# The second feed-forward block's opening tile, half of it in three passes of rounded parts

## The chip, the cores and the metric

The kernel runs on one core of a Trainium2 chip. The metric is the device time of one execution in microseconds (us), taken as the median of several runs. The engines named below are TensorE (PE; its weight loads are listed apart as PEld), VectorE (DVE), ScalarE (ACT), GpSimd (POOL), and SyncE (SP), which here only issues DMA transfers.

## The reference

One inference step of a decoder trunk with one layer: a half-step SwiGLU feed-forward block, a mixer, a second half-step feed-forward block, and a final RMS norm. The width is 1024 features, the hidden width 2816, and 520 tokens go through it (512 of a prompt and 8 single new tokens). Cut to what matters here:

```python
h = h + 0.5 * swiglu(rms_norm(h, ffn1_norm), w1_gate, w1_up, w1_down)
m, states = hybrid_mixer(rms_norm(h, mix_norm), ...)      # ends in  cat @ w_out
h = h + m
h = h + 0.5 * swiglu(rms_norm(h, ffn2_norm), w2_gate, w2_up, w2_down)
y = rms_norm(h, final_norm)
# swiglu(x, wg, wu, wd) = (silu(x @ wg) * (x @ wu)) @ wd
```

All of it is float32.

## The kernel before

**Layout.** Activations lie with features on the 128 partitions: the residual `h` is eight blocks of 128 features by 520 tokens, and the tokens are cut into two halves of 260. So a matmul has a 128x128 weight and moves 260 columns.

**Two kinds of matmul.** Most products are made of rounded parts. A float32 value is split into a rounded part in the type float32r and the rest, also in float32r: ACT makes the first by a copy with a cast, DVE the second by a subtraction (`part`, L250, for activations; `split`, L134, for weights). A product is then three matmuls that add up in PSUM: high weight by high activation, high by low, low by high (`mm3`, L150). A plain product (`plain`, L299) is one float32 matmul of the program on the unsplit values; the trace shows it as two instructions on PE.

**The feed-forward blocks** (`class Ffn`, L271). A hidden tile f is 128 columns of the gate weight and 128 of the up weight. Most tiles are computed by `product` (L470), seven products of sums of quarters instead of eight. They need the activations as seven combinations per pair of feature blocks (j, j+4), j from 0 to 3, each in two parts. For a pair, `scaled` (L229) writes `xg`, four slots of 260 tokens: slots 0 and 3 are the two token halves of block j, slots 1 and 2 those of block j+4. `prep_pair` (L255) makes three DVE instructions of sums (`sums4`, L237: L238, L240, L242), then the parts of slots 0 to 2 in one ACT and one DVE instruction over 780 columns, and the parts of the four sums `xd` over 1040 columns. All go to `xth` and `xtl`; slot 3 itself is not split.

**The opening tile.** The second block's tile 0 (`direct` is 1) is computed by `plain` instead, straight from `xg`, while the mixer's last output projection still runs. Per pair that is eight float32 products: gate and up, block j and block j+4, two token halves. Its gate and up banks are PSUM tiles of the tag BE. Its two weights lie unsplit in one of two 1 MB places `raw`, loaded by `plain_load` (L287). When all four pairs are done, `keep` (L317) copies the banks out.

**The order.** The end of the mixer is written as `LAST_PLAN`, "h0 h2 h1 n0 h3 n1 n2 n3". An `h` step (`wout`, L1292) adds the output projection to two feature blocks of `h`: twelve matmuls to a PSUM bank (eight L160, four L165), one bank per block and token half, two banks in rotation, each added to `h` by one DVE instruction (L1310). As each feature block is complete, `fin` (L782) squares it, and once block j+4 is there it calls `scaled` for pair j. An `n` step (`fill`, L791) emits the eight plain products of pair j and `prep_pair` for that pair. Beyond that, the build works out a fixed order for each engine: it plays the program through on a timeline of its own and lets an instruction that is ready go ahead of an earlier one that is not, unless a line pins it (`keep_in_program_order`, `issue_after`, `high_priority`). So the matmuls of the `n` steps stand between those of the `h` steps on PE.

**After it.** `scales` (L558) makes the token norms, `plain_out` (L365) closes tile 0, and `stream` (L561) runs tiles 1 to 21 and the down projections; for each of them ACT casts and DVE subtracts the weight parts (L139, L141, L396, L400).

Of the kernel before, what the change touches and what calls it, by code (L numbers as in the profile page):

```python
# [10 lines left out]
F32 = mybir.dt.float32  # L11
F32R = mybir.dt.float32r
AF = mybir.ActivationFunctionType
ALU = mybir.AluOpType
# [3 lines left out]
P = 128  # L18
# [4 lines left out]
HB = NT // 2  # L23
HALVES = (slice(0, HB), slice(HB, NT))
KD = D // P
# [43 lines left out]
def tile_trunk_step(ctx: ExitStack, tc: tile.TileContext, ins: dict, outs: dict):  # L69
    nc = tc.nc  # L70
# [7 lines left out]
    tmp = ctx.enter_context(tc.tile_pool(name="tmp", bufs=2, side="right"))  # L78
# [32 lines left out]
    half, ends, added = [], [], []  # L111
# [38 lines left out]
    def mm3(ps, whi, wlo, xhi, xlo, start, stop, pin=False, **kw):  # L150
        first = nc.tensor.matmul(ps, whi, xhi, start=start, stop=False, **kw)  # L151
        if pin:
            tc.keep_in_program_order(first)
        nc.tensor.matmul(ps, whi, xlo, start=False, stop=False, **kw)  # L154
        nc.tensor.matmul(ps, wlo, xhi, start=False, stop=stop, **kw)  # L155
# [11 lines left out]
    def ws(w, k, m=P):  # L167
        return w[:, k * m : (k + 1) * m]
# [60 lines left out]
    def scaled(cell, norm, j, name, halves=False):  # L229
        xg = cell(f"xg_{name}{j}")  # L230
        for d, out in ((j, xg[:, 0::3]), (j + KD // 2, xg[:, 1:3])):
            hd = h[:, d].rearrange("p (b t) -> p b t", b=2)
            for s in (slice(0, 1), slice(1, 2)) if halves else (slice(0, 2),):
                nc.scalar.activation(out=out[:, s], in_=hd[:, s], func=AF.Copy, scale=v(norm, d))
        return xg

    def sums4(xg, xd):  # L237
        nc.vector.tensor_tensor(out=xd[:, 0:2], in0=xg[:, 0::2], in1=xg[:, 3:4].to_broadcast([P, 2, HB]),  # L238
                                op=ALU.subtract)
        nc.vector.scalar_tensor_tensor(out=xd[:, 2], in0=xd[:, 1], scalar=-1.0, in1=xg[:, 0], op0=ALU.mult,  # L240
                                       op1=ALU.subtract)
        return nc.vector.scalar_tensor_tensor(out=xd[:, 3], in0=xd[:, 2], scalar=-1.0, in1=xg[:, 1], op0=ALU.mult,  # L242
                                              op1=ALU.subtract)
# [6 lines left out]
    def part(hi, lo, s):  # L250
        cast = nc.scalar.copy(hi, s)
        low = nc.vector.tensor_tensor(out=lo, in0=s, in1=hi.bitcast(F32), op=ALU.subtract)  # L252
        return cast.ins, low.ins

    def prep_pair(nx, cell, xg, j, name, late=None):  # L255
        xth, xtl, _, _ = nx
        xd = cell(f"xd_{name}{j}")
        last = sums4(xg, xd)

        def parts(s, t):  # L260
            return part(xth[:, j, t], xtl[:, j, t], s)

        parts(xg[:, 0:3], slice(0, 3))
        if late is not None:
            late.append(lambda: parts(xd, slice(3, 7)))
            return None
        return last.ins, *parts(xd, slice(3, 7))
# [3 lines left out]
    class Ffn:  # L271
# [15 lines left out]
        def plain_load(self, f, j=None, us=(0, 1), queue=nc.sync):  # L287
# [3 lines left out]
            for u in us:  # L291
# [4 lines left out]
                     for t in (self.raw[f][:, u], src[2 * f + u]))  # L296
                queue.dma_start(out=next(q), in_=next(q))

        def plain(self, f, xg, j, us=(0, 1), pin=False):  # L299
            for u in us:  # L300
                if (f, u) not in self.banks:
                    n = f"P{self.i}_{f}{u}"
                    if f == 1 and u == 0:
                        bs = [ps[0].tile([P, 512], F32, tag="A", bufs=2, name=f"{n}{b}") for b in range(2)]
                    else:
                        t = ps[0].tile([P, 2, 512], F32, tag="BE", bufs=2, name=n)
                        bs = [t[:, 0], t[:, 1], t]
                    self.banks[f, u] = bs
                for q in range(2):
                    for b, slot in enumerate(((0, 1), (3, 2))):  # L310
                        mm = nc.tensor.matmul(self.banks[f, u][b][:, :HB], ws(self.raw[f][:, u], j + 4 * q),  # L311
                                              xg[:, slot[q]], start=j == q == 0, stop=j == 3 and q == 1,
                                              skip_group_check=True)
                        if pin and q == b == 0:
                            tc.keep_in_program_order(mm)

        def keep(self, f, us):  # L317

# [395 lines left out]
    for j in range(KD // 2):  # L714
# [10 lines left out]
        last = j == KD // 2 - 1  # L725
# [44 lines left out]
    f2 = {}  # L770
# [11 lines left out]
    def fin(d, b, hs):  # L782
# [5 lines left out]
        if j >= 0 and b:  # L788
            f2[j] = scaled(cell2, "ffn2_norm", j, "f2")

    def fill(j):  # L791
        if not j:
            f2["ffn"].plain_load(0)
        f2["ffn"].plain(0, f2[j], j)
        last = j == KD // 2 - 1
        if last:
            with tc.high_priority():
                f2["ffn"].keep(0, (0,))
        f2["ends"] = prep_pair(f2["ffn"].nx, cell2, f2[j], j, "f2")
        if last:  # L800
            with tc.high_priority(), tc.issue_after(f2["ends"][1]):
                f2["copied"] = f2["ffn"].keep(0, (1,))
# [14 lines left out]
    last = act.tile([P, NT], F32, tag="acc", name="acc_last")  # L817
# [674 lines left out]
```

## Time and profile before

| | |
|---|---|
| median of three runs | 953.77 us (952.30 to 954.88) |
| the profiled execution, its own time | 953.41 us |
| its span, first to last instruction | 951.6 us |
| mean granted TensorE clock | 0.997 |
| PE busy | 941.0 us, 7674 matmuls |
| DVE busy | 850.9 us |
| ACT busy | 635.8 us |
| POOL busy | 152.5 us |

The span is read in stages: the first block, the mixer, and the second block from about 613 us on. The stage of the change is the stretch from 575 to 615 us, in which the mixer's last output projection and tile 0 share PE. A line number in a row of the profile is a line of the kernel. In a row of the timeline the columns are the start, the duration, the engine, the line, the operation and what it writes from what it reads; a bracket gives the idle time of the engine before it and what ended that. In the chain of waits the second column is the time that a piece adds to the chain.

### The profile page before, as it was taken

The numbers are of one execution on the slowest core, as the hardware profiler recorded it, in microseconds if no ns is written. First come the engines' busy times: TensorE is split into PE (matmuls) and PEld (weight loads), VectorE is DVE, ScalarE is ACT, GpSimd is POOL, SyncE is SP. The second block draws the span as 40 slices with busy tenths as digits, with TensorE's granted clock in tenths as the row PEclk, the third lists the DMA queues.
The fourth block names the chain that finished last, engine by engine and source line by source line (L and its number), as shares of the span: only waits on it lengthen the run. The fifth ranks groups of instructions, "written<-read, shape, count | busy, mean of one in ns | idle before, by whom it ended". The sixth has DMA issues, their size and how long they took to land.

```text
span 951.6 us, 19687 instructions
## 1 busy us (share of the span) xinstructions
PE 941.0 (99%) x7674; PEld 923.0 (97%) x7674; DVE 850.9 (89%) x1462; ACT 635.8 (67%) x1178; POOL 152.5 (16%) x230
## 2 busy tenths in 40 slices
PE   9999999999999999999999999999999999999996
PEld 8999999999999999999999999999999999999996
DVE  6899899998988698779989998999999999999986
ACT  7787757677566466474768745677776676776764
POOL 0011100100000002146252000112112101122120
PEclk9999999999999999999999999999999999999998
DMA  7676554455553334264365443447766655766652
GB/s 213 179 164 151 145 148 137 117 140 155 136 154 95 86 98 160 91 185 134 97 179 160 122 124 111 124 122 172 174 154 179 167 135 147 175 189 176 158 174 91
DMA packets 54123, 138.36 MB, mean 145 GB/s; under 512 B 7878, under 2 KB 16006, under 8 KB 54030
## 3 DMA queue, kind: packets, MB, share of 16 engines
q1 hardware_dynamic: 40046, 104.20, 34.3%
q0 software_dynamic: 13712, 32.78, 18.5%
q8 instruction: 60, 0.98, 0.4%
q14 instruction: 33, 0.27, 0.1%
q10 hardware_dynamic: 272, 0.13, 0.0%
HBM read 129.74 MB, written 7.34 MB: 144 GB/s over the span
## 4 chain that ended last, share of the span: by engine, by line
PE 79%; DVE 8%; DMA 5%; issue 4%; ACT 2%; POOL 1%; SPq 0%; DVEq 0%; POOLq 0%; ACTq 0%
PE A L160 7%; PE BE L160 6%; PE P L311 4%; PE wo L160 4%; PE A L151 4%; PE A L155 4%; PE A L154 4%; PE A L165 4%; PE BE L165 3%; PE BE L151 3%; PE BE L154 3%; PE BE L155 3%; PE wo L165 2%; PE inz L151 1%; DMA raw<-in_w2gu 1%
## 5 line engine op out<-in xcount | busy, mean ns | idle before, releaser
L504 ACT COPY ac<-A 128x260 f32<-128x260 f32 x85 | 31.7, 373 | 35.8 <-PE A L165 18.1
L433 DVE TENSOR_TENSOR s<-raw 128x1024 f32<-128x1024 f32 x39 | 47.5, 1219 | 5.5 <-DMA raw<-in_w2gu 3.3
L504 ACT COPY ac<-BE 128x260 f32<-128x260 f32 x41 | 15.4, 377 | 33.6 <-PE BE L165 17.9
L151 PE MATMUL inx<-xh_mx,whi_inx 128*128 128x260 f32 x112 | 31.8, 284 | 0.0
L154 PE MATMUL inx<-xl_mx,whi_inx 128*128 128x260 f32 x112 | 31.6, 282 | 0.0
L155 PE MATMUL inx<-xh_mx,wlo_inx 128*128 128x260 f32 x112 | 31.6, 282 | 0.0
L1033 DVE SCALAR_TENSOR_TENSOR A<-U,h,A 128x544 f32<-128x544 f32 x36 | 28.7, 797 | 1.5 <-ACT A L1031 1.1
L311 PE MATMUL P<-x,raw 128*128 128x260 f32 x128 | 28.8, 384 | 0.2 <-DMA raw<-in_w1gu 0.2
L311 PEld LDWEIGHTS P<-x,raw 128*128 128x128 f32 x128 | 24.2, 190 | 4.3 <-DMA raw<-in_w1gu 0.6
L160 PE MATMUL wo<-catg,whi_wo 128*128 128x260 f32 x192 | 27.5, 286 | 0.4 <-DVE h L1310 0.4
L1199 ACT ACTIVATE so<-br,sxdt 128x128 f32<-128x128 f32 x64 | 22.7, 376 | 4.5 <-DVE room L1201 3.2
L160 PEld LDWEIGHTS wo<-catg,whi_wo 128*128 128x128 f32 x192 | 24.8, 188 | 0.8 <-DVE h L1310 0.6
L139 ACT CAST thi<-raw 128x1024 fp32r<-128x1024 f32 (+1 forms) x14 | 14.2, 1013 | 15.6 <-PE wo L160 4.8
L1310 DVE TENSOR_TENSOR h<-wo,h 128x260 f32<-128x260 f32 x48 | 19.2, 420 | 5.5 <-PE wo L165 5.3
L252 DVE TENSOR_TENSOR gs<-gq,gs 128x780 fp32r<-128x780 f32 (+1 forms) x28 | 23.1, 826 | 0.0
L151 PE MATMUL inz<-xh_mx,whi_inz 128*128 128x260 f32 x80 | 22.9, 286 | 0.0
L154 PE MATMUL inz<-xl_mx,whi_inz 128*128 128x260 f32 x80 | 22.7, 283 | 0.0
L155 PE MATMUL inz<-xh_mx,wlo_inz 128*128 128x260 f32 x80 | 22.6, 283 | 0.0
L151 PEld LDWEIGHTS inx<-xh_mx,whi_inx 128*128 128x128 f32 x112 | 21.1, 188 | 0.2 <-issue 0.2
L160 PE MATMUL A<-xth_f,qs 128*128 128x260 f32 x84 | 21.2, 283 | 0.0
L160 PE MATMUL A<-xtl_f,qs 128*128 128x260 f32 x84 | 21.2, 284 | 0.0
L155 PEld LDWEIGHTS inx<-xh_mx,wlo_inx 128*128 128x128 f32 x112 | 21.1, 188 | 0.0
(3135 smaller groups left out, 4373.4 us busy)
## 6 DMA issues: line engine op xcount, KB each, us to landing
raw<-in_w2gu SPq DMA_DIRECT2D x44, 512.0 KB, 4.4
raw<-in_w1gu SPq DMA_DIRECT2D x41, 512.0 KB, 4.3
raw<-in_w_in SPq DMA_DIRECT2D x24, 512.0 KB, 3.5
raw<-in_w1d SPq DMA_DIRECT2D x16, 512.0 KB, 5.0
raw<-in_w2d SPq DMA_DIRECT2D x16, 512.0 KB, 4.6
raw<-in_w_out SPq DMA_DIRECT2D x12, 512.0 KB, 3.6
ab<-scr_acs SPq DMA_DIRECT2D x8, 512.0 KB, 5.9
h<-in_state_ssm SPq DMA_DIRECT2D x16, 256.0 KB, 3.9
```

Of the source, the lines that this page charges most:

```text
L151: first = nc.tensor.matmul(ps, whi, xhi, start=start, stop=False, **kw)
L154: nc.tensor.matmul(ps, whi, xlo, start=False, stop=False, **kw)
L155: nc.tensor.matmul(ps, wlo, xhi, start=False, stop=stop, **kw)
L160: mm = nc.tensor.matmul(ps, w, x, start=start, stop=False, **kw)
L165: nc.tensor.matmul(ps, w, xhi[k], start=False, stop=k == len(wlo) - 1, **kw)
L252: low = nc.vector.tensor_tensor(out=lo, in0=s, in1=hi.bitcast(F32), op=ALU.subtract)
L311: mm = nc.tensor.matmul(self.banks[f, u][b][:, :HB], ws(self.raw[f][:, u], j + 4 * q), xg[:, slot[q]], start=j == q == 0, stop=j == 3 and ...
L433: nc.vector.tensor_tensor(out=s1, in0=diag, in1=up0, op=ALU.add)
L504: self.copied = nc.scalar.copy(keep, out[:, :HB]).ins
L1033: nc.vector.scalar_tensor_tensor(out=A[:, :n], in0=U[:, j : j + n], scalar=w(j), in1=A[:, :n], op0=ALU.mult, op1=ALU.add)
L1199: nc.scalar.activation(out=o[:, q], in_=br, func=AF.Copy, scale=sxdt[:, j, b : b + 1]))
L1310: nc.vector.tensor_tensor(out=h[:, d, hs], in0=ps[:, :HB], in1=h[:, d, hs], op=ALU.add)
```

## The change

For pairs 0 and 1 the eight products of tile 0 become products of rounded parts; pairs 2 and 3 stay plain. Five things change in the program:

- `weight_parts` splits the first two 128-blocks of each weight quarter (a tile of 128x4x256) into `w0h` and `w0l`: one ACT cast and one DVE subtraction over 1024 columns, right behind the load.
- For pairs 0 and 1 `prep_pair` stands ahead of the products instead of behind them, since the products now read `xth` and `xtl` for slots 0 to 2.
- Slot 3 gets parts of its own, `x3h` and `x3l` (260 columns each, tag `ta`, of which there are two buffers in all).
- `parts_plain` makes the eight products with `mm3`: 24 float32r matmuls for the pair, into the same banks.
- `plain_banks` is the allocation of the banks, taken out of `plain`.

```diff
+        def parts_plain(self, f, w, x3, j):
+            self.plain_banks(f, (0, 1))
+            for u in range(2):
+                for q in range(2):
+                    wh, wl = (t[:, 2 * u + q, j * P : j * P + P] for t in w)
+                    for b, slot in enumerate(((0, 1), (3, 2))):
+                        xh, xl = x3 if slot[q] == 3 else (t[:, j, slot[q]] for t in self.nx[:2])
+                        mm3(self.banks[f, u][b][:, :HB], wh, wl, xh, xl, j == q == 0, False, skip_group_check=True)
+
         def plain(self, f, xg, j, us=(0, 1), pin=False):
+            self.plain_banks(f, us)
+            for u in us:
+                for q in range(2):
+                    for b, slot in enumerate(((0, 1), (3, 2))):
+                        mm = nc.tensor.matmul(self.banks[f, u][b][:, :HB], ws(self.raw[f][:, u], j + 4 * q),
+                                              xg[:, slot[q]], start=j == q == 0, stop=j == 3 and q == 1,
+                                              skip_group_check=True)
+                        if pin and q == b == 0:
+                            tc.keep_in_program_order(mm)
+
+        def plain_banks(self, f, us):
             for u in us:
                 if (f, u) not in self.banks:
...
                     self.banks[f, u] = bs
-                for q in range(2):
-                    for b, slot in enumerate(((0, 1), (3, 2))):
-                        mm = nc.tensor.matmul(self.banks[f, u][b][:, :HB], ws(self.raw[f][:, u], j + 4 * q),
-                                              xg[:, slot[q]], start=j == q == 0, stop=j == 3 and q == 1,
-                                              skip_group_check=True)
-                        if pin and q == b == 0:
-                            tc.keep_in_program_order(mm)
...
+    def weight_parts():
+        src = f2["ffn"].raw[0].rearrange("p u (q c) -> p (u q) c", q=2)[:, :, : 2 * P]
+        hi, lo = (f2["xg"].tile([P, 4, 2 * P], F32R, tag=t, name=t) for t in ("w0h", "w0l"))
+        nc.scalar.copy(hi, src)
+        nc.vector.tensor_tensor(out=lo, in0=src, in1=hi.bitcast(F32), op=ALU.subtract)
+        f2["w0"] = hi, lo
+
     def fill(j):
+        ffn, last = f2["ffn"], j == KD // 2 - 1
         if not j:
-            f2["ffn"].plain_load(0)
-        f2["ffn"].plain(0, f2[j], j)
-        last = j == KD // 2 - 1
+            ffn.plain_load(0)
+            weight_parts()
+        if j < 2:
+            prep_pair(ffn.nx, cell2, f2[j], j, "f2")
+            x3 = [tmp.tile([P, HB], F32R, tag="ta", name=f"{t}{j}") for t in ("x3h", "x3l")]
+            part(*x3, f2[j][:, 3])
+            ffn.parts_plain(0, f2["w0"], x3, j)
+            return
+        ffn.plain(0, f2[j], j)
         if last:
             with tc.high_priority():
-                f2["ffn"].keep(0, (0,))
-        f2["ends"] = prep_pair(f2["ffn"].nx, cell2, f2[j], j, "f2")
+                ffn.keep(0, (0,))
+        f2["ends"] = prep_pair(ffn.nx, cell2, f2[j], j, "f2")
```

## The prediction

> **What bounds the kernel now.** I read the page first, for the engine that carries the span.
>
> ```profile
> span 951.6 us, 19687 instructions
> PE 941.0 (99%) x7674; PEld 923.0 (97%) x7674; DVE 850.9 (89%) x1462; ACT 635.8 (67%) x1178; POOL 152.5 (16%) x230
> PEclk9999999999999999999999999999999999999998
> PE 79%; DVE 8%; DMA 5%; issue 4%; ACT 2%; POOL 1%; SPq 0%; DVEq 0%; POOLq 0%; ACTq 0%
> ```
>
> PE is busy for 941.0 of 951.6 us at the full granted clock, and four fifths of the chain that ended last are PE. DVE at 850.9 us is the only engine near it. So a microsecond taken from PE counts unless DVE cannot follow. That is decided in the stage of the change, so next I read the busy time by stretches around it (us, then PE, PEld, DVE, ACT, POOL busy).
>
> ```profile
> 575.00:583.20 8.20, 7.77 (x65) 7.55 (x64) 6.03 (x11) 3.51 (x5) 0.00 (x0) 1.00 0.40 130
> 583.20:603.60 20.40, 20.40 (x140) 19.23 (x139) 16.60 (x28) 13.26 (x18) 4.13 (x5) 1.00 0.55 137
> 603.60:614.60 11.00, 11.00 (x71) 10.18 (x70) 10.89 (x17) 9.43 (x14) 0.85 (x1) 1.00 0.47 109
> 614.60:636.00 21.40, 21.40 (x180) 21.34 (x179) 21.37 (x29) 16.19 (x27) 1.70 (x2) 1.00 0.41 113
> ```
>
> PE never pauses from 583.2 to 636. DVE has 2.17 us free before 583.2 and 3.80 us up to 603.6, but 0.11 us from there to 614.6 and 0.03 us in the 21.4 us after. The room on DVE ends at 603.6; whatever the change adds must be done before. ACT has room throughout.
>
> **What PE saves.** The groups of PE's instructions from 583 to 614 us give the opening tile's share, and the chain of waits in the same stretch gives what each instruction really takes of PE's time (the mean of 382 ns overlaps its neighbours).
>
> ```profile
> L311 PE MATMUL P<-xg_f,raw 128*128 128x260 f32 x64 | 15.0, 382 | 0.0
> ```
>
> ```profile
> 583.38 1.75 PE P L311 x8
> 585.13 0.95 PE wo L160 x8
> 586.08 0.48 PE wo L165 x4
> ...
> 587.99 3.51 PE P L311 x16
> ```
>
> There are 64 instructions for 4 pairs of 8 products, so two to a product. Sixteen take 3.51 us: 219 ns each, 439 ns a product. The output projection's matmuls are of the kind that the change puts in, float32r by 260 columns with a weight load each: twelve take 0.95 + 0.48 = 1.43 us, 119 ns each, so a product in three passes takes 358 ns. A product becomes 81 ns cheaper, and two pairs have 16: **1.29 us off PE**. Nothing else on PE goes or comes.
>
> [...]
>
> **What ACT and DVE get.** The added instructions and their nearest rows, first of ACT and then of DVE, by the timeline:
>
> ```profile
> 578.72 0.72 ACT L234 ACTIVATE xg_f<-h 128x520 f32<-128x520 f32 x1
> 580.09 1.05 ACT L139 CAST whi_wo<-raw 128x1024 fp32r<-128x1024 f32 x1 [0.65 <-PE wo L160]
> 581.62 0.72 ACT L234 ACTIVATE xg_f<-h 128x520 f32<-128x520 f32 x1
> 585.17 0.85 ACT L251 CAST xth_f<-xg_f 128x780 fp32r<-128x780 f32 x1
> 588.24 0.61 ACT L246 CAST qs<-raw 128x512 fp32r<-128x512 f32 x1
> ```
>
> ```profile
> 581.17 1.22 DVE L141 TENSOR_TENSOR wlo_wo<-raw,whi_wo 128x1024 fp32r<-128x1024 f32 x1 [0.18 <-ACT whi_wo L139]
> 582.92 0.92 DVE L1310 TENSOR_TENSOR h<-wo,h 128x260 f32<-128x260 f32 x2
> 587.16 0.69 DVE L238 TENSOR_TENSOR xd_f<-xg_f 128x520 f32<-128x520 f32 x1
> 587.77 0.96 DVE L252 TENSOR_TENSOR xtl_f<-xg_f,xth_f 128x780 fp32r<-128x780 f32 x1
> 588.99 0.42 DVE L240 SCALAR_TENSOR_TENSOR xd_f<-xd_f,xg_f 128x260 f32<-128x260 f32 x1
> 591.40 0.42 DVE L242 SCALAR_TENSOR_TENSOR xd_f<-xd_f,xg_f 128x260 f32<-128x260 f32 x1
> 599.03 0.43 DVE L1310 TENSOR_TENSOR h<-wo,h 128x260 f32<-128x260 f32 x1 [1.00 <-PE wo L165]
> ```
>
> The weight parts are one cast of 1024 columns, 1.05 us, and one subtraction, 1.22 us. Slot 3 costs each pair a cast and a subtraction of 260 columns. The cast has no row of that size; from 780 columns at 0.85 and 512 at 0.61 a straight line gives 0.38, and it lies between nothing and 0.61; I take 0.38. The subtraction I take at 0.42, as L240. So **ACT gets 1.05 + 2 x 0.38 = 1.81 us and DVE 1.22 + 2 x 0.42 = 2.06 us**. The moved `prep_pair` is the same work at another place, and it issues no DMA; no queue of SP or POOL is passed.
>
> Is there cover? DVE must do 2.06 us more in a stage that PE makes 1.29 us shorter: 3.35 us against the 3.80 + 2.17 = 5.97 us that stand free up to 603.6. These are waits for PE, like the 1.00 us before the row at 599.03, so they can be used. ACT must find 1.81 + 1.29 = 3.10 of 20.40 - 13.26 = 7.14 us. Both fit, DVE with 2.6 us over. If part of it does not fit, it reaches DVE's closed stretch and comes back as lateness of weight parts. Here is the nearest place where that would bite, tile 4:
>
> ```profile
> 644.12 1.22 DVE L141 TENSOR_TENSOR slo_4d<-raw,shi_4d 128x1024 fp32r<-128x1024 f32 x1
> 646.53 0.55 PEld L165 LDWEIGHTS A<-xth_f,slo_4d 128*128 128x128 f32 x4
> ```
>
> DVE ends at 645.34 and PE takes the weights at 646.53: 1.19 us to spare. If DVE from 603.6 on does not come earlier at all, PE can come 1.19 us earlier, not 1.29. That is my value: **1.19 us net**, with 1.29 above it; the end below is all of DVE's addition lost, worked out in the first rival.
>
> **What the products now wait for.** Before, the first eight instructions of tile 0 needed `xg` of block 0 alone, ready at 578.72 + 0.72 = 579.44:
>
> ```profile
> 583.22 1.92 PE L311 MATMUL P<-xg_f,raw 128*128 128x260 f32 x8
> ```
>
> ```profile
> 567.38 8.58 SPq L293 DMA_DIRECT2D raw<-in_w2gu  x2
> ```
>
> Now pair 0's products need both blocks of `xg` (581.62 + 0.72 = 582.34), and behind that on DVE, in the order of the program, the sums (0.69 + 0.42 + 0.42), the parts of slots 0 to 2 (0.96) and of slot 3 (0.42), the weight parts (1.22), whose raw weights are loaded until after 575.96, and the two additions to `h` that stood there (0.92). Together 5.05 us: about 587.4, and 4.2 us later than the 583.22 of before. I cost this delay at nothing, because PE has other work: ten more banks of the output projection (one block of h2, two each of h1 and h3, two halves each) at 1.43 us, 14.3 us in all, whose last weights DVE finished at 582.39. Without that cover it costs up to 4.2 us. Pair 1 has a wait of its own: `x3h` and `x3l` fill both buffers of their tag, so the cast of pair 1's slot 3 must wait for the last product of pair 0, and behind it on ACT wait the casts of later pairs. That is one cast and one subtraction, 0.80 us, which one bank of the projection (1.43 us) covers.
>
> **The sum.** The profiled execution took 953.41 us, 1.81 more than its span, and the median is 0.36 above it. 953.41 - 1.19 = 952.22; by the median, 953.77 - 1.19 = **952.6 us**.
>
> **The rivals.** About 0.3% (2.86 us) is what a measurement of this kernel can tell from no change.
>
> *DVE takes it back.* Nothing of the 2.06 us is absorbed, since the free time lies at the wrong moments in an order fixed beforehand. Then DVE is 2.06 us late and PE 1.29 early at tile 4; with 1.19 us to spare PE waits 2.16 us there, and the net is +0.87 us: 954.6. For it speaks the full DVE from 603.6 on; against it, that the new work is due before 590 and the largest piece depends only on a load. I give it 0.16.
>
> *PE stands before pair 0.* This is the one that ends slower. In the fixed order the 24 matmuls of pair 0 keep the place at 583.2 that the plain ones had, or one soon after, and PE's queue waits for DVE: 4.2 us at full price, and the 0.80 us of pair 1 with it, less the 1.29 saved: +3.7 us, 957.5. It turns the saving over from 1.29 us of standing still on, and passes 0.3% from 4.15 us on. For it: only two banks rotate in the projection, so PE runs ahead of DVE by little. Against it: the order in the trace follows readiness, since tile 0's 64 instructions are already cut into pieces between banks, as the chain shows. I give it 0.10. [...]
>
> *The order is dealt anew to advantage.* Later in the block PE waits at two places:
>
> ```profile
> 738.67 0.75 PE L165 MATMUL A<-xth_f,slo_9d 128*128 128x260 f32 x4 [0.57 <-DVE slo_9d L141]
> ...
> 878.46 0.39 PE L160 MATMUL BE<-xth_f,shi_19c 128*128 128x260 f32 x1 [0.75 <-ACT BE L504]
> ```
>
> Both hang on transfers and on DVE's order, which a shift can move. If both went, 1.29 + 0.57 + 0.75 = 2.61 us: 951.2. A shift can as well make them longer. I give it 0.09.
>
> *It doesn't do what it says.* Were a pass of the new matmuls as dear as half a plain product, 16 x (657 - 439) ns would be +3.5 us, 957.3. The projection's 119 ns in the same place speak against it: 0.02.
>
> **How the numbers follow.** The forecast keeps 0.63. Its own range is the 1.19 us give or take the spread of the runs shown (1.1 to 1.5 us about the median), 951.4 to 953.9. The whole range takes in the better order and DVE's loss with the same spread, 951.0 to 955.4, and leaves out the standing PE and the last. Faster by over 0.3% needs the better order and some luck of the measurement: 0.06. Slower by over 0.3% is most of the standing PE, the last, and a little of DVE's loss: 0.11. The same: 0.83.
>
> **What would show it.** The end of the stage is PE's sum of squares:
>
> ```profile
> 612.29 1.04 PE L210 MATMUL psr_f<-acc_f,ones 128*128 128x260 f32 x4
> ```
>
> Right: 32 instructions of L311 for the second block instead of 64, 48 new matmuls at about 119 ns, PE full from 583 to 614, and this row about 1.3 us earlier than 612.29. DVE's free time up to 603.6 shrinks by about 3 us. The first product of pair 0 stands behind more banks of the projection, near 587. Wrong: an idle PE row before a product of pair 0 or 1 that names DVE; a wait for tile 4's low weights longer than 0.1 us; or a second block whose instructions stand in a wholly different order, which would make the sum of single terms worthless.

## The result and the profile after

The changed kernel takes 956.00 us (954.57 to 957.65, ten runs) beside 953.19 us for the kernel before (952.24 to 954.88, ten runs): a ratio of 1.0033, with an interval of 1.0024 to 1.0041. By the medians it is slower by 2.8 us, where 1.2 us less was forecast. Measured once more on another occasion, below, the ratio was 1.0020 (1.0009 to 1.0031): slower both times, there by 1.6 us.

The changed kernel's page gives the span, the engines and the chain that ended last.

```profile
span 953.4 us, 19730 instructions
PE 941.8 (99%) x7690; PEld 925.5 (97%) x7690; DVE 853.7 (90%) x1465; ACT 637.5 (67%) x1181; POOL 151.9 (16%) x230
PE 94%; DVE 3%; ACT 2%; issue 1%; DMA 0%; DVEq 0%; ACTq 0%; SPq 0%
```

PE was to be busy 1.3 us less and is busy 0.8 us more, at a chain that is almost all PE. Nothing here tells where. The stretches that the prediction looked at do (us, then PE, PEld, DVE, ACT, POOL busy, granted clock, DMA share, GB/s):

```profile
575.00:583.20 8.20, 7.76 (x65) 7.55 (x64) 5.38 (x9) 3.03 (x5) 0.00 (x0) 1.00 0.44 130
583.20:603.60 20.40, 18.05 (x135) 17.73 (x134) 17.25 (x29) 13.54 (x20) 3.22 (x4) 0.92 0.41 104
603.60:614.60 11.00, 11.00 (x77) 10.38 (x76) 9.21 (x18) 7.97 (x12) 1.77 (x2) 1.00 0.44 97
614.60:636.00 21.40, 21.11 (x165) 20.46 (x164) 21.37 (x28) 15.55 (x26) 0.85 (x1) 1.00 0.52 141
```

In the second row PE, which never paused there before, stands for 2.35 us, and the clock is 0.92 where it was 1.00. PE's timeline shows the place.

```profile
583.64 0.64 PE L165 MATMUL wo<-catg,tlo 128*128 128x260 f32 x4
586.62 1.51 PE L160 MATMUL wo<-catg,thi 128*128 128x260 f32 x8 [2.35 <-DVE h L1337]
587.94 1.07 PE L165 MATMUL wo<-catg,tlo 128*128 128x260 f32 x4
588.80 1.94 PE L160 MATMUL wo<-catg,thi 128*128 128x260 f32 x8
590.54 0.75 PE L165 MATMUL wo<-catg,tlo 128*128 128x260 f32 x4
591.13 1.12 PE L160 MATMUL wo<-catg,whi_wo 128*128 128x260 f32 x8
```

The stop is ahead of the first matmuls of block 5, whose PSUM bank the addition of block 4 must free first. No product of the opening tile is at the stop. Before, the first eight matmuls of the plain products stood between these two banks (583.22, 1.92 us). Behind the stop the 24 matmuls of block 5 take 4.51 us (586.62 to 591.13) where 24 at 119 ns are 2.9. The windows of 2 us say why: the number after POOL's is the granted clock.

```profile
586.00:588.00 2.00, 1.38 (x9) 1.38 (x10) 1.29 (x4) 1.06 (x2) 0.00 (x0) 0.84 0.59 174
588.00:590.00 2.00, 2.00 (x11) 2.00 (x11) 1.27 (x4) 1.04 (x2) 0.00 (x0) 0.50 0.22 88
590.00:592.00 2.00, 2.00 (x16) 2.00 (x16) 2.00 (x3) 1.19 (x3) 0.00 (x0) 0.81 0.01 4
592.00:594.00 2.00, 2.00 (x20) 2.00 (x19) 2.00 (x6) 2.00 (x4) 0.85 (x1) 1.00 0.78 227
```

What held the addition back is read from the queues of ACT and DVE, in the order in which they work:

```profile
580.76 1.05 ACT L807 CAST w0h<-raw 128x1024 fp32r<-128x1024 f32 x1 [5.13 <-DMA raw<-in_w2gu]
583.00 0.41 ACT L251 CAST x3h<-xg_f 128x260 fp32r<-128x260 f32 x1
583.32 1.04 ACT L139 CAST whi_wo<-raw 128x1024 fp32r<-128x1024 f32 x1
```

```profile
581.84 1.23 DVE L808 TENSOR_TENSOR w0l<-raw,w0h 128x1024 fp32r<-128x1024 f32 x1 [2.82 <-ACT w0h L807]
583.45 0.43 DVE L252 TENSOR_TENSOR x3l<-xg_f,x3h 128x260 fp32r<-128x260 f32 x1
584.39 1.23 DVE L141 TENSOR_TENSOR wlo_wo<-raw,whi_wo 128x1024 fp32r<-128x1024 f32 x1 [0.18 <-ACT whi_wo L139]
585.54 0.69 DVE L204 TENSOR_TENSOR acc_f<-acc_f,sq_f 128x520 f32<-128x520 f32 x1
586.15 0.76 DVE L1337 TENSOR_TENSOR h<-wo,h 128x260 f32<-128x260 f32 x2
```

The cast of the weight parts stands at the head of ACT's queue for 5.13 us, until the second half of the raw weights has landed. The squares and the cast of the next output weights wait behind it, on DVE the subtractions behind those, and the two additions to block 4, last in that line, come at 586.15. Before they came at 582.92.

To hold kernels apart from the scatter of earlier and later stages I use one length, **the stage**: from the first matmul of `wo<-catg,thi` near 562 us to the first load of tile 2's low weights (`A<-xth_f,slo_2d`). It is 65.54 us before (562.27 to 627.81) and 69.06 us after (563.15 to 632.21): 3.52 us longer. Up to the added cast the orders of all engines are the same in both kernels, so the later start, 0.88 us, is not the change's; what comes behind the stage took 323.8 us before and 321.2 after, and between 321 and 325 in the kernels below. Such differences are scatter: one and the same kernel, run twice below as adds_first and adds_first_b, began its stage at 563.88 and at 562.38 us and took 321.5 and 323.9 us behind it.

### The profile page after: what moved, and what is told of

It is laid out like the page before. It is cut to its first block, busy times and chain, and to the rows that moved or that the text cites. A ratio compares the mean times of both kernels' runs of the same rounds, so it can differ in the third digit from the quotient of the medians.

```text
span 953.4 us, 19730 instructions
## 1 busy us (share of the span) xinstructions
PE 941.8 (99%) x7690; PEld 925.5 (97%) x7690; DVE 853.7 (90%) x1465; ACT 637.5 (67%) x1181; POOL 151.9 (16%) x230
## 4 chain that ended last, share of the span: by engine, by line
PE 94%; DVE 3%; ACT 2%; issue 1%; DMA 0%; DVEq 0%; ACTq 0%; SPq 0%
PE A L160 8%; PE BE L160 6%; PE A L165 4%; PE A L151 4%; PE A L155 4%; PE A L154 4%; PE wo L160 4%; PE P L313 3%; PE BE L165 3%; PE BE L151 3%; PE BE L155 3%; PE BE L154 3%; PE wo L165 2%; PE inx L151 2%; PE inx L154 2%; PE inx L155 2%
```

## The experiments

All times are medians, ratios are to runs of before that were measured together with the kernel. "Stage" is the change of that length against 65.54 us. A stop of 0.43 us near 576 us is in every kernel and is left out. The last column has the stops that the profile reports; gaps inside its merged rows come on top and make up to about 0.9 us of a stage (in after_b PE's busy time in the stage is 64.69 us against 65.11 before, 0.42 less, where 1.29 us of work was saved). A table first, then each kernel.

| kernel | time, us | ratio (interval) | stage, us | longest stops of PE in it |
|---|---|---|---|---|
| after | 956.00 | 1.0033 (1.0024 to 1.0041) | +3.52 | 2.35, and the clock at 0.50 |
| late | 954.49 | 1.0014 (1.0006 to 1.0023) | +0.91 | 1.00 |
| wparts_only | 953.34 | 1.0005 (0.9995 to 1.0014) | +0.59 | none |
| wait_only | 952.73 | 1.0003 (0.9993 to 1.0013) | 0.00 | none |
| warm | 957.49 | 1.0047 (1.0035 to 1.0059) | +2.92 | 1.70 |
| pair1 | 956.42 | 1.0031 (1.0019 to 1.0043) | +2.29 | 0.94, 0.47, 0.38 |
| pairs12 | 955.40 | 1.0027 (1.0014 to 1.0041) | +2.61 | 1.31, 0.95, 0.47 |
| pairs12_late | 956.21 | 1.0031 (1.0019 to 1.0043) | +2.19 | 1.62, 0.64, 0.41 |
| late_dma | 953.32 | 1.0003 (0.9993 to 1.0013) | +0.56 | 0.81, 0.22 |
| unread | 955.80 | 1.0021 (1.0009 to 1.0033) | +1.59 | 0.95 |
| tick | 956.31 | 1.0031 (1.0019 to 1.0044) | +3.90 | 2.56, and the clock at 0.50 |
| late_dma2 | 953.61 | 1.0015 (1.0005 to 1.0024) | +0.94 | 1.63 |
| tick2 | 957.63 | 1.0050 (1.0033 to 1.0067) | +4.90 | 3.07, and the clock at 0.50 |
| adds_first | 954.71 | 1.0018 (1.0004 to 1.0032) | +0.12 | 1.12 |
| after_b | 954.92 | 1.0020 (1.0009 to 1.0031) | +2.27 | 2.34, the clock at 1.00 |
| adds_first_b | 954.09 | 1.0005 (0.9994 to 1.0016) | +0.08 | 1.07 |

Theory: the loss is the stop ahead of block 5, made by the wait on ACT and the new work on DVE that stand ahead of the additions, now that no product is there to fill it. Rivals: the added work on DVE and ACT by itself, wherever it stands; the later readiness of pair 0; and the clock as a loss of its own.

**late.** The changed kernel with the weight parts held back: the cast behind the last `xg` of pair 0 on ACT, the subtraction behind the additions of block 4 on DVE.

```diff
-            weight_parts()
+            with queued(last_xg["f2", 0], last_add[2, KD // 2, 1]):
+                weight_parts()
```

> The changed kernel with one edit: the cast of the weight parts is queued on ACT behind the last xg of pair 0, and their subtraction on DVE behind the addition to h of block 4, instead of wherever the order puts them. Theory 1, the held queues: the cast stands at the head of ACT's queue and waits 5.1 us for the load of raw; behind it wait the squares and xg on ACT and the additions to h on DVE, so PE stops 2.35 us for a bank and then runs at a lower clock. It expects the 5.1 us of ACT gone, less than 0.5 us of waiting on PE before the block-5 bank, the clock at 1.00 throughout the stage, and 951.5 to 952.6 us, that is the 1.2 to 1.3 us of the products below the kernel before. Theory 2, no filler: the plain products of pair 0 used to fill PE while DVE freed a bank, and the new ones are ready too late for that. It expects PE to stand 1.5 us or more at the same place still, and 955 us or more. Theory 3, too much work for DVE: the 2.06 us come back later; 954.5 to 955.5 us.

The wait on ACT is gone and the clock stays at 1.00. The stop ahead of block 5 is down to about 0.16 us, but another of 1.00 us comes three banks later.

```profile
584.30 1.22 PE L161 MATMUL wo<-catg,thi 128*128 128x260 f32 x8
590.12 1.22 PE L161 MATMUL wo<-catg,whi_wo 128*128 128x260 f32 x8 [1.00 <-DVE h L1339]
```

```profile
587.03 1.22 DVE L447 TENSOR_TENSOR s<-raw 128x1024 f32<-128x1024 f32 x1
588.16 1.22 DVE L809 TENSOR_TENSOR w0l<-raw,w0h 128x1024 fp32r<-128x1024 f32 x1
589.30 0.42 DVE L241 SCALAR_TENSOR_TENSOR xd_f<-xd_f,xg_f 128x260 f32<-128x260 f32 x1
589.64 0.42 DVE L1339 TENSOR_TENSOR h<-wo,h 128x260 f32<-128x260 f32 x1
```

The moved subtraction stands ahead of another addition. Most of the loss is gone with the wait: 0.91 us of stage is left, from 3.52 in after, or from 2.27 in the profile of after_b, in which the clock did not fall. The rest is the same mechanism at a smaller size. The time, 954.49 us, lies above the 951.5 to 952.6 that the first theory named and at the edge of the third's range.

**wparts_only** and **wait_only.** The kernel before with the weight parts added and read by nobody, over all 1024 columns, and over 4.

```diff
+            weight_parts()                       # wparts_only: [:, :, : 2 * P];  wait_only: [:, :, :1]
```

> The kernel before plus the weight parts alone, made at the same place as in the changed kernel and read by nobody; the products stay plain. Theory 1: ACT waits about 5 us at the cast and DVE 2 to 3 us at the subtraction, the additions to h come late, and PE waits; the plain products of pair 0 cover part of it. 954.0 to 955.5 us against some 953.2 of before. Theory 2: the filler is in its place, so no change, 952.9 to 953.5. Theory 3: up to 1.2 us, without a wait on ACT having to do with it.

> The kernel before plus the wait alone: at the place of the weight parts a cast and a subtraction of one column of each weight quarter (4 columns), read by nobody. It has the wait for the load, and next to none of the work. Theory 1: ACT waits as long as with the whole parts, and about half or more of the loss of that kernel is here, 953.6 to 955.0 us. Theories 2 and 3: no change, 952.9 to 953.5.

ACT waits in both, 4.93 and 4.37 us, and the profile reports no stop of PE in either. In wparts_only:

```profile
579.56 1.05 ACT L794 CAST w0h<-raw 128x1024 fp32r<-128x1024 f32 x1 [4.93 <-DMA raw<-in_w2gu]
580.64 1.23 DVE L795 TENSOR_TENSOR w0l<-raw,w0h 128x1024 fp32r<-128x1024 f32 x1 [2.63 <-ACT w0h L794]
583.10 1.92 PE L311 MATMUL P<-xg_f,raw 128*128 128x260 f32 x8
584.97 1.22 PE L160 MATMUL wo<-catg,thi 128*128 128x260 f32 x8
```

The eight matmuls of plain products cover the same lateness of the additions. (The 0.59 us of wparts_only are two small gaps, ahead of the matmuls at 584.97 and 596.33, whose weight loads wait 0.36 and 0.50 us for an addition.) So at this place the wait alone costs nothing measurable, nor does the missing filler alone (late: 0.16 us); the 2.35 us need both.

**warm.** The changed kernel with ten small matmuls on PE ahead of block 5's bank, to keep the clock up.

```diff
+            if (j, d) == (2, 5):
+                busy = e["ps"][0].tile([P, 512], F32, tag="A", bufs=2, name="busy")
+                for _ in range(10):
+                    tc.keep_in_program_order(nc.tensor.matmul(busy[:, :P], e["ones"], e["ones"], start=True, stop=True))
```

> The changed kernel plus ten small matmuls of ones, read by nobody, on PE ahead of the bank of block 5, where it stood still; some 2.2 us of PE time. They do not shorten the wait, they fill it. If the lower clock behind the wait (0.50 to 0.84 of full over 6 us) is a cost of its own, the clock stays at 1.00 and the time falls by 1.2 to 1.7 us below the changed kernel, to 954.3 to 954.8. If it is not, the time stays within 0.5 us of the changed kernel, 955.5 to 956.5.

It did not isolate the clock: the order was dealt anew, pair 0 came right behind block 5, and PE stood there as the prediction's slower rival has it, for 1.70 us at an unchanged clock.

```profile
590.00 0.39 PE L154 MATMUL P<-xtl_f,w0h 128*128 128x260 f32 x1 [1.70 <-DVE xtl_f L252]
```

**pair1, pairs12, pairs12_late.** Other pairs are rounded, so that the plain products of pair 0 stay as filler: pair 1 alone; pairs 1 and 2; and these two with the weight parts held back as in late.

```diff
-        if j < 2:
+        if 1 <= j < 2:          # pairs12 and pairs12_late: 1 <= j < 3
```

> The changed kernel with rounded parts for pair 1 alone; pair 0 is plain again, as before, and so are pairs 2 and 3. The weight parts are half as large (512 columns) but stand where they stood, so the wait for the load stays. The joined theory: the held queue and the missing filler are one loss, each alone costs little, since eight plain products of pair 0 (1.75 us for their first half) cover the lateness of the additions to h. It expects ACT to wait 4 to 5 us all the same, PE to wait under 0.3 us before the block-5 bank, the clock at 1.00, and 0.64 us saved on products less what DVE's 1.1 us cost: 952.0 to 953.3 us against 952.8 of before. If the held queue alone were the cause: PE stands 1 us or more there, 954 us or more.

> The changed kernel with rounded parts for pairs 1 and 2 instead of 0 and 1; the weight parts as large as there and at the same place. As many products in three passes, so 1.29 us less on PE, with pair 0 plain as a filler. The joined theory expects no standing still before the block-5 bank, and 951.5 to 953.0 us unless pair 2, which now stands at the end of the stage, has PE wait for its parts there; that would show as waits for DVE after 606 us and 953 to 954.5 us. The theory of the held queue alone: 955 us or more.

> As the kernel with pairs 1 and 2, and the weight parts queued behind the last xg of pair 0 (ACT) and the addition to h of block 4 (DVE), so neither the held queue nor the missing filler is left. The joined theory expects it level with its twin within 0.6 us, 951.5 to 953.3 us, since with the filler in place the wait costs little.

All three were expected near or below before and are 2.1 to 3.1 us above it by the medians. The stop ahead of block 5 is gone or down to 0.38 us, but PE now stands for the rounded products themselves and for additions behind their parts. The largest, in pairs12_late:

```profile
609.53 0.39 PE L155 MATMUL P<-xtl_f,w0h 128*128 128x260 f32 x1 [1.62 <-DVE xtl_f L253]
```

So the filler of pair 0 is not the only thing lost. A plain product needs `xg` alone; a rounded one needs what DVE makes last for its pair, and for none of pairs 0, 1 and 2 was DVE early enough. Pair 3 was not tried.

**late_dma** and **late_dma2.** As late, but ACT writes the negative of the high parts and a transfer from POOL's queue adds the raw weights to it, so DVE is spared 1.22 us. In late_dma2 the negative copy is made from the raw weights, ahead of the cast.

```diff
-        nc.vector.tensor_tensor(out=lo, in0=src, in1=hi.bitcast(F32), op=ALU.subtract)
+        nc.scalar.activation(out=lo, in_=hi.bitcast(F32), func=AF.Copy, scale=-1.0)   # late_dma2: in_=src
+        for u in range(2):
+            nc.gpsimd.dma_start(out=lo[:, 2 * u : 2 * u + 2], in_=home[:, u, :, : 2 * P], accum_op=ALU.add)
```

> The kernel with the late weight parts (pairs 0 and 1), but the low weight parts made by ACT and an accumulating transfer of POOL's queue instead of DVE's 1.22 us. In the late kernel PE waits 1.00 us for an addition to h that stands behind that subtraction. If DVE's added work is what is left of its loss, the time falls by 0.8 to 1.3 us below it, to 953.2 to 953.7 us; if the missing filler is, it stays at 954 to 955.

> As late_dma, but the negative copy for the low weight parts is taken from the raw columns ahead of the high parts, so the accumulating transfer starts over 1 us earlier. Theory (late_dma gave back the saving of 1.29 us in two stops of TensorE, 0.22 us for the additions and 0.81 us for the transfer's landing): the stop for the landing is gone, and the time is 952.3 to 953.0 with before at 953.3. Rival (another stop of the same size takes its place, since the products of pairs 0 and 1 still wait for parts made on ACT and DVE): 953.2 to 954.0.

Without the 1.22 us on DVE the 1.00 us stop of late shrinks to 0.22, and the kernel is level with before. What it keeps of the 1.29 us goes to a wait for the transfer. Starting the transfer earlier let the order take the products earlier too, and that wait grew; the second half landed 7.1 us after its issue.

```profile
593.66 0.36 PE L156 MATMUL P<-xth_f,w0l 128*128 128x260 f32 x1 [0.81 <-DMA w0l<-in_w2gu]
```

```profile
594.31 0.39 PE L156 MATMUL P<-xth_f,w0l 128*128 128x260 f32 x1 [1.63 <-DMA w0l<-in_w2gu]
```

**unread.** The kernel before with all of the new work on ACT and DVE, `prep_pair` ahead of the products, and plain products throughout; the new parts are read by nobody.

```diff
+        if j < 2:
+            prep_pair(f2["ffn"].nx, cell2, f2[j], j, "f2")
+            x3 = [tmp.tile([P, HB], F32R, tag="ta", name=f"{t}{j}") for t in ("x3h", "x3l")]
+            part(*x3, f2[j][:, 3])
+            f2["ffn"].plain(0, f2[j], j)
+            return
```

> All the new work on ACT and DVE is done (weight parts, rounded last group, the preparation of pairs 0 and 1 ahead of their products) at the places of the changed kernel, but nobody reads the weight parts and the last group's parts: the products of pairs 0 and 1 stay plain float32, so they wait for no part. Work is added, none is left out. Theory (the loss is that the products lost their freedom: plain ones need only the scaled columns and the raw load, and so filled TensorE while DVE was late): the eight plain products stand between the banks of blocks 4 and 5 again, no stop over 0.5 us there, and only the tail is later, by 0.6 us: 953.3 to 954.2 against about 953.2 of before. Rival (ACT's 1.8 us and DVE's 2.1 us more, and the preparation moved forward, are the loss, whoever reads them): a stop of 1 us or more before a bank of the stage and 955 to 956.5.

PE does not stop ahead of block 5, as the theory had it. But it stops for 0.95 us farther on, which the rival named, because the parts of pairs 0 and 1 now stand ahead of an addition:

```profile
596.60 1.23 DVE L252 TENSOR_TENSOR xtl_f<-xd_f,xth_f 128x1040 fp32r<-128x1040 f32 x1
597.75 0.41 DVE L1324 TENSOR_TENSOR h<-wo,h 128x260 f32<-128x260 f32 x1
```

```profile
598.22 1.22 PE L160 MATMUL wo<-catg,whi_wo 128*128 128x260 f32 x8 [0.95 <-DVE h L1324]
```

So both hold. The added and moved work costs 1.59 us of stage (and 2.8 us of the medians, 955.80 against 952.97) even when nobody reads it: more than the 1.29 us that the products save. The theory that the missing filler is all of the loss is too narrow.

**tick** and **tick2.** The changed kernel with one matmul of eight columns on the squares of block 4, meant to part the stop; in tick2 it is also pinned to its place.

```diff
+                if (j, d, b) == (2, 5, 0):
+                    tick = e["ps"][0].tile([P, 512], F32, tag="A", bufs=2, name="tick")
+                    tc.keep_in_program_order(nc.tensor.matmul(
+                        tick[:, :8], e["ones"], e["last_sq"]["f2", 4][:, :8], start=True, stop=True))
```

> The changed kernel with one matmul more, of eight columns of the squares of block 4, which ScalarE has ready about 0.7 us into the 2.35 us for which TensorE stood idle before block 5's bank; the order of every other instruction is that of the changed kernel. Theory (one unbroken stop of over 2 us let the granted clock fall, and that cost 1.64 us more): the two halves of the stop are about 0.7 and 1.5 us, the clock stays at 1.00 in the 2-us windows from 586 on, and the stage is about 1.6 us shorter: 954.2 to 954.7. Rival (the clock follows the share of busy time, or the fall was an accident of one profiled run): it falls to about 0.5 again and the time is 955.6 to 956.4, or it doesn't fall and the time is still 955.6 to 956.4.

> The small matmul on the squares of block 4 again, now held to its place between the banks of blocks 4 and 5, so that it falls into the stop and parts it. The products of pair 0 come right behind block 5 in this kernel, as in warm, so its whole time is not what is asked; the question is what the 24 matmuls of block 5 take behind the parted stop. Theory (one unbroken stop of over 2 us lowers the granted clock): two stops of about 0.7 and 1.5 us, the clock at 1.00, and 2.9 to 3.0 us from block 5's first matmul to the next bank or product, where the changed kernel took 4.51. Rival (the clock follows the idle time summed up, or the share of busy time): 4.3 to 4.6 us again, with windows at 0.5 to 0.8. The time, with the stop of warm before pair 0 besides: 956.0 to 957.5 if the clock stays, 957.0 to 959.0 if it falls.

Neither parted it. I had taken the square at 584.30 for block 4's; it is block 1's, and block 4's can only come behind the additions that PE waits for. In tick the small matmul slid behind block 5, in tick2 it made the stop longer. Both show the fall of the clock again; in tick2 block 5 ran at 0.50 up to 592 us and beyond, and the time is 4.7 us above before.

```profile
588.00:590.00 2.00, 2.00 (x11) 2.00 (x11) 1.44 (x3) 0.48 (x1) 0.00 (x0) 0.50 0.01 4
```

```profile
587.42 0.59 PE L1338 MATMUL tick<-sq_f,ones 128*128 128x8 f32 x2 [3.07 <-ACT sq_f L205]
```

**adds_first.** The changed kernel with one DVE instruction moved: the subtraction for the last output weights stands behind the two additions of block 4.

```diff
+        if (j, d2) == (2, 3):
+            behind[j, d2] = (e["last_add"][2, 4, 1],)
```

> The changed kernel with one DVE instruction moved: the subtraction for the low parts of the last unit of output weights, 1.23 us, stands behind the two additions of block 4 for which TensorE stopped, not ahead of them. ScalarE's wait for the raw load and all of the new work stay. Theory (TensorE's stop is the time for which DVE's queue holds the additions back, and the lower granted clock comes only behind a stop of over 1.7 us): the additions then wait only for the sum of squares that still stands ahead of them, which can't start before its square from ScalarE at about 584.95, so the stop shrinks from 2.35 to about 1.75 us; the clock stays at 1.00 or falls for less than 2 us, and the 24 matmuls of block 5 take 2.9 to 3.4 us, not 4.51: 953.9 to 955.0. Rival (the stop and the fall of the clock don't hang on this queue, or the moved subtraction stops TensorE later by as much): a stop as long at another place, and 955.6 to 956.4.

The wait on ACT (4.46 us) and all added work stay. The stop is 1.12 us, less than the 1.75 expected, the clock stays at 1.00, and the stage is 0.12 us longer than before.

```profile
585.02 0.70 DVE L205 TENSOR_TENSOR acc_f<-acc_f,sq_f 128x520 f32<-128x520 f32 x1 [0.75 <-ACT sq_f L204]
585.64 0.76 DVE L1340 TENSOR_TENSOR h<-wo,h 128x260 f32<-128x260 f32 x2
586.31 1.22 DVE L142 TENSOR_TENSOR wlo_wo<-raw,whi_wo 128x1024 fp32r<-128x1024 f32 x1
```

```profile
586.11 1.22 PE L161 MATMUL wo<-catg,thi 128*128 128x260 f32 x8 [1.12 <-DVE h L1340]
```

One instruction of 1.2 us, ahead of an addition or behind it, moves the stage by 3.4 us. Of these, 1.23 are the shorter stop itself, about 1.5 the clock that did not fall, and 0.65 come behind the sum of squares: from pair 0's products on the build dealt a new order to PE, so that last piece can't be put down to the one instruction alone.

**after_b** and **adds_first_b.** The changed kernel and adds_first, both unaltered, side by side, since the runs of adds_first lay between 951.97 and 959.35 us.

> The changed kernel unaltered, on the same chip and beside the same runs of before as the next kernel. Either theory: 2.3 to 3.6 us over before, and the stage 3.5 us longer with the stop of about 2.4 us and the lower clock behind it.

> The changed kernel with the one subtraction behind the two additions, unaltered from adds_first, whose stage was 0.12 us longer than in before but whose runs scattered over 7 us. Theory (the stop and the lower clock were the loss, and what the runs of adds_first showed beyond that is scatter of later stages): 952.6 to 954.0 where before takes 953.2, and at least 2 us less than the changed kernel beside it. Rival (the loss comes back in later stages whatever the stage does): 954.8 to 956, within 1.3 us of the changed kernel beside it.

By the medians they differ by 0.83 us, so not by the 2 us that I had asked for; adds_first_b is level with before (953.35), and the changed kernel is not. The profile of after_b shows one reason why the changed kernel's own runs scatter: the same orders on all engines, the same stop, of 2.34 us, and this time no fall of the clock.

```profile
587.11 1.25 PE L160 MATMUL wo<-catg,thi 128*128 128x260 f32 x8 [2.34 <-DVE h L1337]
588.19 0.65 PE L165 MATMUL wo<-catg,tlo 128*128 128x260 f32 x4
588.67 1.11 PE L160 MATMUL wo<-catg,thi 128*128 128x260 f32 x8
589.62 0.64 PE L165 MATMUL wo<-catg,tlo 128*128 128x260 f32 x4
590.10 1.11 PE L160 MATMUL wo<-catg,whi_wo 128*128 128x260 f32 x8
```

Block 5 takes 2.99 us (587.11 to 590.10), not 4.51, and the stage is 2.27 us longer, not 3.52. So the clock's part, about 1.5 us, comes in some executions and not in others, at the same stop; what decides it no run shows.

## Why the prediction was wrong

**What PE saves: right.** In the profile after, the 24 matmuls of pair 0 take 2.86 us (592.56 to 595.42), 119 ns each. As eight plain products, by the prediction's row, they were 3.51, so a pair saves 0.65 and two save the 1.29 us of the sum.

**What ACT and DVE get: right in size.** Cast and subtraction of slot 3 took 0.41 and 0.43 us, of the weights 1.05 and 1.23: 1.87 us on ACT and 2.09 on DVE, where 1.81 and 2.06 were forecast.

**"Is there cover?": this step failed.** It set 3.35 us against 5.97 us of free time on DVE up to 603.6 and found room. Each engine works through one order, and what counts is not how much time is free but what stands behind the new instructions. Behind the weight parts stood the additions that give PE its banks, and PE had a lead of a bank or so on them. Nor was the free time all waits for PE, as the prediction read it: of the 3.80 us up to 603.6, DVE waited 0.70 us for ACT's square (ahead of 584.55) and 0.77 for a load (ahead of 586.02). In after DVE still had 20.40 - 17.25 = 3.15 us free in the stretch where PE lost 2.35 us to it. The unread kernel prices the step: the same work, read by nobody, costs 1.59 us of stage, where the prediction had put nothing beyond 0.10 us at tile 4.

**The wait that the change adds: not named.** The prediction knew that the raw weights are still being loaded when the cast is due, and let pair 0 wait for them. It did not ask what is queued behind the cast on ACT: 5.13 us of waiting ahead of the squares and of the next output weights. That the largest piece "depends only on a load" was even counted in its favour.

**"I cost this delay at nothing, because PE has other work": this failed too.** The ten banks of the output projection were no cover, since each needs an addition by DVE, the engine that is late. The cover was what the change removed: plain products ask nothing of DVE beyond the additions that had long made their `h`, and they stood in the place where PE runs ahead of the additions. Pair 0's own products came at 592.56 us, not near 587. wparts_only and wait_only, with that filler, stand the same wait without a stop.

**The sum, as the profiles show it.** Up to the sum of squares (`psr_f`) the stage of after is 2.88 us longer: -1.29 saved, +2.35 for the stop, 5.94 - 36 x 0.119 = +1.66 for the 36 matmuls behind it (586.62 to 592.56), nearly all of it the lower clock, and 0.16 in small gaps. Behind it come 0.64 us more, 0.29 of it a wait of tile 1 for the parts that `prep_pair` now makes later:

```profile
619.13 0.39 PE L160 MATMUL BE<-xtl_f,shi_1c 128*128 128x260 f32 x1 [0.29 <-DVE xtl_f L252]
```

That is +3.52. In after_b, without the fall of the clock, it is +2.27: -1.29, +2.34 for the stop, 0.62 in small gaps (0.33 of them where pair 0 waits for `xtl_f`), and 0.60 behind.

**The rivals.** "DVE takes it back" had the engine right and the place wrong: tile 4 has 1.17 us to spare, as before, and PE does not wait there. "PE stands before pair 0" is not what happened in the changed kernel, where pair 0 had slipped behind three more banks, but it is what warm shows, at 1.70 us, and, before pairs 1 and 2, the pairs12 kernels, at up to 1.62. The order dealt to advantage can't be told from scatter: the waits at 738 and 878 us are gone in the profile of after, but such waits come and go among the kernels above (unread has the first again, at 743, and two others at 733 and 740; late has none of them). The matmuls cost what they should, so "doesn't do what it says" is out. What came, a time more than 0.3% above before (1.0033), had been given a chance of 0.11, and by the second measurement (1.0020) it would not have been over 0.3%.

**What stays open.** No kernel parted the stop, so whether a parted one would have kept the clock up was not tried; nor do the traces show why it fell behind the stop of 2.35 us in after and not behind that of 2.34 in after_b. And adds_first, with its stage level, ran 0.7 to 1.1 us above before by the medians; whether that is scatter of later stages the intervals don't say. No version beat the kernel before: late_dma and adds_first_b are level with it.

## What to carry to other kernels

Free time of an engine that works through one order is no cover (in after DVE had 3.15 us free in the stretch in which PE lost 2.35 to it): write down which instruction of the bound engine waits for the next thing in that queue, and add the new work, and the wait at its head, to that. Before replacing work on the bound engine by cheaper work, ask what the old work needed; instructions that need nothing of a nearly full engine are filler, and their worth is the stops that they hide, not their own duration (the first eight matmuls of the plain products, 1.92 us of PE, stood where PE now stops for 2.35). An instruction that waits for a load, and work that waits for it, goes behind, not ahead of, what the next engine is short of: the weight parts held back (late) took the stage from 3.52 us over (2.27 without the fall of the clock) to 0.91, and one subtraction moved behind two additions (adds_first) to 0.12.

## What the runs showed of the hardware

The granted clock of TensorE fell to 0.50 behind stops of 2.35 us (after) and 2.56 (tick) and in one of 3.07 (tick2); behind a stop of 2.34 us in after_b, the same kernel as after, it did not fall, nor behind those of 1.70 (warm), 1.63 (late_dma2) and 1.62 (pairs12_late). The windows of 2 us tell when it changed. In after, 0.84 over 586 to 588 us puts the fall at 587.36, and 0.81 over 590 to 592 puts the rise at 590.76. In tick the clock was low from 586.64 to 590.04, in tick2 from 586.36 to 593.20: twice 3.4 us, and once 6.8. In after the fall came 0.74 us behind the end of the stop (586.62), in tick 0.61 us behind it (586.03), and in tick2 1.06 us ahead of it (587.42).

So no length of a stop can be named from which on the clock falls: 2.35 us brought the fall and 2.34 did not, and why is not shown. The theory of tick and tick2, that one unbroken stop of over 2 us lowers the clock, was an estimate from the 2.35 us of after and the 1.70 of warm; after_b speaks against it as a rule. With the fall, a stop of 2.35 us cost about 4.0 us (2.35 + 1.66).
